# Differential attention's scores on two row halves of the array, memory heads' keys and values in two places

## The chip, the core and the metric

The kernel runs on one core of one Trainium2 chip. The metric is the device time of one execution in microseconds, median of the runs; the program is launched once and all its inputs lie in the chip's memory. Five engines work side by side: TensorE (PE in the profile, its weight loads PEld), VectorE (DVE), ScalarE (ACT), GpSimd (POOL) and SyncE (SP), which here issues most transfers. Each works through its own list of instructions in order and waits on semaphores for the others.

## What is computed

One step of a two-layer encoder with 1024 prompt frames and 32 sample frames, width 1024. Layer 0 mixes tokens by causal pooling, layer 1 by differential attention; each layer also attends, with four heads, to 256 memory tokens, and ends with a squared-ReLU feed-forward part of width 4096. The change is in layer 1. Its differential attention, four heads with two components of 64 dimensions each, in the reference:

```python
def diff_core(q, k, v, q_pos, k_pos, lam, slopes):
    s = jnp.einsum('bqhcd,bkhcd->cbhqk', q, k).astype(jnp.float32) * (DIFF_HEAD_DIM ** -0.5)
    dist = jnp.abs(q_pos[:, None] - k_pos[None, :]).astype(jnp.float32)
    bias = -slopes[:, None, None] * dist[None]
    vis = (k_pos[None, :] // CHUNK) <= (q_pos[:, None] // CHUNK)
    s = jnp.where(vis, s + bias, -jnp.inf)
    p = jax.nn.softmax(s, axis=-1)
    a = p[0] - lam * p[1]
    return jnp.einsum('bhqk,bkhe->bqhe', a.astype(v.dtype), v)
```

The memory attention is a plain softmax attention over 256 keys of 128 dimensions:

```python
def mem_attend(q, k, v):
    s = jnp.einsum('bthd,bmhd->bhtm', q, k).astype(jnp.float32) * (MEM_HEAD_DIM ** -0.5)
    p = jax.nn.softmax(s, axis=-1).astype(v.dtype)
    return jnp.einsum('bhtm,bmhd->bthd', p, v).reshape(B, T, MEM_WIDTH)
```

## The kernel before

Everything is held transposed: features on the 128 partitions, frames along the free dimension. The 1056 frames are three groups of 352 (`GW`). To keep accuracy, each operand of a matmul is split into a high part, rounded to the format F32R, and a low part, the rest (`split`, L56 and L57: a cast by ACT and a subtraction by DVE or POOL). A product is then three matmuls, high by high, low by high and high by low (`mm3`, L51 to L53).

Layer 1's attention is `mix1`. A main list of work (`diff_unit`, then `mem_unit`) is driven against a filler, `fill1`, which projects keys, values and queries of the coming heads; `drive` lets so much of the filler run after each step as the step's `yield` says, so that TensorE has dense matmuls while the softmax of a block is under way. The tile framework then sets the order on each engine.

Scores of differential attention (`diff_scores`): a head's 1024 queries come in 8 blocks of 128 (index `i`, two to a `pair`), against the first `Wi` keys, 256 to 1024. Before the change a component's 64 dimensions fill all 128 rows of the array: the tile KS holds, for component `c`, the high part of the keys on one half of the partitions and the low part on the other, and Q holds the queries' high part on both halves, and likewise the low part. Two matmuls of 128 rows (L799 and L800) so give all four products of the parts. The copies of Q on the other half are made by transfers issued by SP (L734), two for each 256 queries. Each component takes a score tile of its own (`sctile`, two banks of accumulator memory, two such tiles), one after the other, with a `yield` between. DVE adds the distance table and takes the minimum (L806), ACT takes the exponential (L808), ACT and DVE combine the two components (L779, L780); component 1 has a single buffer (`p1`).

`diff_values` transposes the combined probabilities in TensorE (L841), splits them (tiles aTh and aTl) and multiplies them with the split values V, three matmuls for each 128 keys in the order of `mm3`.

Memory heads (`mem_unit`): `mem_load_kv` loads a head's keys into `mkr`, splits them into `mk`, loads its values into the same `mkr` (named mvr), and splits them into `mv`. `mkr`, `mk` and `mv` have one place each. The matmuls on them are `sc<-mk,mq` and `mm<-aTh,mv` at L51 to L53.

The sample group has its own small attention (`diff_sample`): scores at L878 and L879 with 64 rows and 32 columns of the array, values at L902 (128 rows) and L903 (32 rows).

The functions that the change touches, with the profile's line numbers:

Of the kernel before, what the change touches and what calls it, by code (L numbers as in the profile page):

```python
# [9 lines left out]
F32 = mybir.dt.float32  # L10
F32R = mybir.dt.float32r
AF = mybir.ActivationFunctionType
ALU = mybir.AluOpType
# [3 lines left out]
SEQ = 1024  # L17
NS = 32
NT = SEQ + NS
GW = 352  # L20
# [7 lines left out]
SC_DIFF = 64.0 ** -0.5  # L28
# [7 lines left out]
KEYS_AT = 1  # L36
T2_AT, T_AT = 8, 20
# [5 lines left out]
class Kern:  # L43
# [211 lines left out]
    def setup_late(self, b):  # L255
        nc, t = self.nc, self.t
        self.dtab = b.tile([128, 1152], F32, name="dtab")
        self.dists = b.tile([128, 288], F32, name="dists")
        self.claim(b, (("os", 512, 2),))
        nc.sync.dma_start(self.dists, t["dists"])  # L260
# [75 lines left out]
    def mem_project(self, l, h, p, out, qs, gate=()):  # L336
        nc = self.nc
# [4 lines left out]
        for g in range(NG):  # L342
# [4 lines left out]
            for a, lo, hi in ((0, 0, 512), (1, 512, SEQ)):  # L347
                lo, hi = max(lo, g * GW), min(hi, (g + 1) * GW)
                if lo < hi:
                    s = slice(lo - 512 * a, hi - 512 * a)  # L350
                    self.split(q[a][:, 0, s], q[a][:, 1, s], qf[:, lo - g * GW:hi - g * GW], nc.gpsimd)
            if g == NG - 1:
                nc.gpsimd.tensor_copy(qs[:, h, :], qf[:, GW - NS:])
        out[h] = q

# [329 lines left out]
    def diff_project(self, h, p, out, smp):  # L685
        nc, t = self.nc, self.t
# [23 lines left out]
        Q = []  # L710
        for g in range(NG):
# [4 lines left out]
            lo, end = g * GW, min((g + 1) * GW, SEQ)  # L716
            if h:
                yield from self.until(("s", h - 1, (end - 1) // 256))
            while lo < end:
                n = lo // 256  # L720
                hi = min(end, 256 * (n + 1))
                s = slice(lo - 256 * n, hi - 256 * n)
                if len(Q) == n:
                    Q.append(self.qp.tile([128, 2, 2, 256], F32R, tag="q", name="Q", bufs=self.nq))
                q = Q[n]
# [13 lines left out]
    def diff_keys(self, h, smp):  # L739
# [6 lines left out]
        KSf = KS.bitcast(F32)  # L746
        for a in range(4):
            s = slice(256 * a, 256 * a + 256)
            nc.scalar.copy(KS[0:64, 0, s], kst[0:64, s])
            nc.scalar.copy(KS[64:128, 1, s], kst[64:128, s])  # L750
            nc.vector.tensor_tensor(KS[64:128, 0, s], kst[0:64, s], KSf[0:64, 0, s], ALU.subtract)
            nc.vector.tensor_tensor(KS[0:64, 1, s], kst[64:128, s], KSf[64:128, 1, s], ALU.subtract)
            yield 0.0
# [28 lines left out]
    def diff_scores(self, h, pair, p, d, A):  # L782
        nc = self.nc
        Wk = 256 * (pair + 1)
        q = d["Q"][pair]
        KS = self.KS[h]
        for i in (2 * pair, 2 * pair + 1):
            qc = slice((i % 2) * 128, (i % 2) * 128 + 128)
            Wi = max(256, 128 * (i + 1))
            st = self.pd.tile([128, 8], F32, tag="std", name="std", bufs=4)  # L790
            prs = []
            for c in range(2):
                tile = self.sctile()
                n = Wi if Wi <= 512 else Wi // 2
                off = 512 - n if Wi > 512 else 0
                sc = tile[:, off:off + Wi]
                for k in range(0, Wi, n):
                    o = sc[:, k:k + n]
                    nc.tensor.matmul(o, lhsT=q[:, c, 0, qc], rhs=KS[:, c, k:k + n], start=True, stop=False)  # L799
                    nc.tensor.matmul(o, lhsT=q[:, c, 1, qc], rhs=KS[:, c, k:k + n], start=False, stop=True)  # L800
# [10 lines left out]
                if c == 0:  # L811
                    yield 0.22 * (pair + 1)
# [868 lines left out]
```

## Time and profile before

| what | us |
|---|---|
| median of 3 runs | 2105.55 (2105.54 to 2108.3) |
| profiled execution, its own time | 2107.0 |
| span of its profile, first to last instruction | 2105.2 |
| TensorE busy in the span | 2081.7 (99%) |
| DVE, ACT, POOL busy | 1683.4, 1125.7, 568.0 |
| mean granted TensorE clock | 0.997 |
| layer 1's score matmuls, first start | 1015.6 |
| layer 1's score matmuls, last start | 1228.3 |
| memory heads' last value product of layer 1 | 1324.9 |

A row of the page's part on groups gives line, engine, operation, the tile written and those read, the form (rows x columns), the count, busy time and mean duration, and behind the last bar the idle time ahead of it with what ended it. The timeline gives start and duration of single instructions; in a matmul's row the form `64*32 64x256` reads: 64 rows and 32 columns of the array in use, 256 columns streamed. Matmul records overlap, so the pace is read from starts.

### The profile page before, as it was taken

To read this page: it belongs to the slowest core of one execution; us is meant where nothing else is said; L and a number is where in the kernel's file an instruction comes from. 1 tells how busy PE (TensorE), PEld (TensorE's weight loads), DVE (VectorE), ACT (ScalarE), POOL (GpSimd) and SP (SyncE) were. 2 spreads that over 40 slices of the span, in tenths; PEclk is the share of its full clock that TensorE was granted. 3 is DMA by queue.
4 is the path that set the end of the run, shared out by engine and by line. 5 is a ranking of instruction groups with operands and counts; after the bars stand their busy time and mean duration, and the time that the engine had idled before them with its cause. 6 is when DMAs were issued, how large, how long until landed. Compare 5 with 4: busy or idle time off the path is not lost. (4 is left out here: it accounts for less than half of the span.)

```text
span 2105.2 us, 35352 instructions
## 1 busy us (share of the span) xinstructions
PE 2081.7 (99%) x13068; PEld 2045.3 (97%) x13068; DVE 1683.4 (80%) x3164; ACT 1125.7 (53%) x2437; POOL 568.0 (27%) x577
## 2 busy tenths in 40 slices
PE   9999999999999999999999999999999999999998
PEld 8998999999999999999999998999999999999997
DVE  8856598888888888868778877589888888888865
ACT  7546365444444444456777766355544444444454
POOL 1021113333333333220111212104334333333323
PEclk9999999999999999999999999999999999999999
DMA  5634411111111111124222213411111111111112
GB/s 192 198 113 139 149 55 56 51 49 53 49 53 45 57 41 60 41 71 159 77 79 79 83 37 99 160 51 51 56 46 54 48 51 51 48 53 50 52 41 83
DMA packets 88269, 156.85 MB, mean 75 GB/s; under 512 B 12832, under 2 KB 30880, under 8 KB 87584
## 3 DMA queue, kind: packets, MB, share of 16 engines
q1 hardware_dynamic: 86224, 149.61, 22.3%
q10 hardware_dynamic: 1872, 4.98, 0.8%
q8 instruction: 102, 1.67, 0.3%
q14 instruction: 71, 0.58, 0.1%
HBM read 126.64 MB, written 23.72 MB: 71 GB/s over the span
## 5 line engine op out<-in xcount | busy, mean ns | idle before, releaser
L51 PE MATMUL dn<-xh,whi 128*128 128x352 f32 x1168 | 383.8, 329 | 2.9 <-ACT xh L229 1.1
L52 PE MATMUL dn<-xl,whi 128*128 128x352 f32 x1168 | 379.0, 324 | 0.4 <-DVE xl L230 0.4
L53 PE MATMUL dn<-xh,wlo 128*128 128x352 f32 x1168 | 378.9, 324 | 0.0
L109 DVE TENSOR_TENSOR wlo<-wraw,whi 128x512 fp32r<-128x512 f32 x344 | 280.1, 817 | 83.6 <-ACT whi L108 82.8
L1375 DVE TENSOR_TENSOR x<-x,mm 128x352 f32<-128x352 f32 x560 | 287.5, 513 | 62.7 <-PE mm L53 62.6
L108 ACT CAST whi<-wraw 128x512 fp32r<-128x512 f32 x344 | 212.4, 620 | 232.4 <-PE dn L52 117.5
L51 PE MATMUL mm<-h2h,whi 128*128 128x352 f32 x832 | 270.4, 325 | 0.0
L53 PE MATMUL mm<-h2h,wlo 128*128 128x352 f32 x832 | 268.0, 322 | 0.0
L52 PE MATMUL mm<-h2l,whi 128*128 128x352 f32 x832 | 266.4, 320 | 0.0
L108 ACT CAST whi<-ws 128x512 fp32r<-128x512 f32 x232 | 143.9, 620 | 220.3 <-PE dn L52 123.4
L1375 DVE TENSOR_TENSOR x<-x,xb 128x352 f32<-128x352 f32 x448 | 222.8, 511 | 26.1 <-PE xb L53 23.4
L51 PEld LDWEIGHTS dn<-xh,whi 128*128 128x128 f32 x1168 | 219.8, 188 | 8.4 <-issue 2.0
L52 PEld LDWEIGHTS dn<-xl,whi 128*128 128x128 f32 x1168 | 221.0, 189 | 3.1 <-DVE xl L230 1.3
L53 PEld LDWEIGHTS dn<-xh,wlo 128*128 128x128 f32 x1168 | 220.4, 189 | 0.4
L57 POOL TENSOR_TENSOR h2l<-t,h2h 128x352 fp32r<-128x352 f32 x112 | 137.0, 1224 | 170.8 <-ACT h2h L56 170.8
L109 DVE TENSOR_TENSOR wlo<-ws,whi 128x512 fp32r<-128x512 f32 x232 | 179.0, 772 | 3.5 <-ACT whi L108 3.5
L57 POOL TENSOR_TENSOR h2l<-b,h2h 128x352 fp32r<-128x352 f32 x92 | 116.2, 1275 | 228.7 <-PE mm L53 204.0
L1359 POOL TENSOR_TENSOR t<-b,b 128x352 f32<-128x352 f32 x56 | 64.7, 1155 | 366.3 <-ACT b L1278 366.3
L52 PEld LDWEIGHTS mm<-h2l,whi 128*128 128x128 f32 x832 | 156.3, 188 | 0.4
L51 PEld LDWEIGHTS mm<-h2h,whi 128*128 128x128 f32 x832 | 156.1, 188 | 0.4
L53 PEld LDWEIGHTS mm<-h2h,wlo 128*128 128x128 f32 x832 | 156.2, 188 | 0.0
L53 PE MATMUL dn<-T,wlo 128*128 128x352 f32 x480 | 155.7, 324 | 0.0
(312 smaller groups left out, 5326.9 us busy)
## 6 DMA issues: line engine op xcount, KB each, us to landing
wraw<-in_w_ff SPq DMA_DIRECT2D x256, 256.0 KB, 2.6
wraw<-in_w_out SPq DMA_DIRECT2D x44, 256.0 KB, 3.6
wraw<-in_w_mem SPq DMA_DIRECT2D x32, 256.0 KB, 3.1
wraw<-in_w_in SPq DMA_DIRECT2D x30, 256.0 KB, 3.1
o<-oscr SPq DMA_DIRECT2D x36, 176.0 KB, 3.0
xscr<-x SPq DMA_DIRECT2D x3, 1408.0 KB, 4.7
wraw<-in_w_kv SPq DMA_DIRECT2D x16, 256.0 KB, 2.6
Q<-Q SPq DMA_DIRECT2D x32, 128.0 KB, 2.2
```

Source lines behind the costliest of these rows:

```text
L51: mm(ps, lhsT=ah, rhs=bh, start=first, stop=False, skip_group_check=more)
L52: mm(ps, lhsT=ah, rhs=bl, start=False, stop=False, skip_group_check=more)
L53: self.last_mm = mm(ps, lhsT=al, rhs=bh, start=False, stop=last, skip_group_check=more)
L57: (lo_eng or self.nc.vector).tensor_tensor(lo, src, hi.bitcast(F32), ALU.subtract)
L108: self.nc.scalar.copy(hi, src)
L109: eng.tensor_tensor(lo, src, hi.bitcast(F32), ALU.subtract)
L1359: self.nc.gpsimd.tensor_tensor(h[out], h[a], h[c], ALU.subtract)
L1375: nc.vector.tensor_tensor(xj, xj, ps, ALU.add)
```

## The change

Each component's 64 dimensions now use one half of the array's rows: component 0 rows 0 to 63, component 1 rows 64 to 127. KS and Q hold high and low part as two planes of all 128 partitions, split like any other operand, by ACT and DVE in pieces of 512 columns for the keys, by ACT and POOL for the queries (`split_q`, which the memory queries use too). The copies of Q by SP are gone. A block has three matmuls of 64 rows a component (high by high, high by low, low by high), issued in turn for component 0 and 1, without a `yield` between. Up to 512 keys both components share a score tile, one bank each; above, both tiles are taken at once. A head's queries take two tiles of 512 and not four of 256, and the filler may be two heads ahead (`until` on head h - 2).

In `diff_values` the three products go by part: all that need the high part of the probabilities first. `mk` and `mv` have two places in layer 1 (`nmk`). The sample group's distance table is loaded where it is used and not ahead, and the weights of two `yield`s change (0.22 to 0.25).

```diff
+    def split_q(self, q, qf, g):
+        for a, lo, hi in ((0, 0, 512), (1, 512, SEQ)):
+            lo, hi = max(lo, g * GW), min(hi, (g + 1) * GW)
+            if lo < hi:
+                s = slice(lo - 512 * a, hi - 512 * a)
+                self.split(q[a][:, 0, s], q[a][:, 1, s], qf[:, lo - g * GW:hi - g * GW], self.nc.gpsimd)
...
     def diff_project(self, h, p, out, smp):
...
-        Q = []
+        if h > 1:
+            yield from self.until(("s", h - 2, 3))
+        Q = [self.qp.tile([128, 2, 512], F32R, tag="q", name="Q", bufs=self.nq) for a in range(2)]
...
-                for c in range(2):
-                    b = slice(64 * c, 64 * c + 64)
-                    self.split(q[b, c, 0, s], q[b, c, 1, s], qf[b, lo - g * GW:hi - g * GW], nc.gpsimd)
-                lo = hi
-                if hi == 256 * (n + 1):
-                    qd = q.bitcast(F32)
-                    for c in range(2):
-                        b, o = slice(64 * c, 64 * c + 64), slice(64 - 64 * c, 128 - 64 * c)
-                        nc.sync.dma_start(qd[o, c], qd[b, c])
+            self.split_q(Q, qf, g)
...
     def diff_keys(self, h, smp):
...
-        for a in range(4):
-            s = slice(256 * a, 256 * a + 256)
-            nc.scalar.copy(KS[0:64, 0, s], kst[0:64, s])
-            nc.scalar.copy(KS[64:128, 1, s], kst[64:128, s])
-            nc.vector.tensor_tensor(KS[64:128, 0, s], kst[0:64, s], KSf[0:64, 0, s], ALU.subtract)
-            nc.vector.tensor_tensor(KS[0:64, 1, s], kst[64:128, s], KSf[64:128, 1, s], ALU.subtract)
+        for a in range(0, SEQ, 512):
+            s = slice(a, a + 512)
+            self.split(KS[:, 0, s], KS[:, 1, s], kst[:, s])
...
     def diff_scores(self, h, pair, p, d, A):
...
+            n = Wi if Wi <= 512 else Wi // 2
+            if Wi > 512:
+                sc = [self.sctile()[:, 512 - n:512 - n + Wi] for c in range(2)]
+            else:
+                tile = self.sctile()
+                sc = [tile[:, 512 * c:512 * c + Wi] for c in range(2)]
+            for k in range(0, Wi, n):
+                for m, (u, v) in enumerate(((0, 0), (0, 1), (1, 0))):
+                    for c in range(2):
+                        b = slice(64 * c, 64 * c + 64)
+                        nc.tensor.matmul(sc[c][:, k:k + n], lhsT=q[b, u, qc], rhs=KS[b, v, k:k + n],
+                                         start=m == 0, stop=m == 2)
             prs = []
             for c in range(2):
-                tile = self.sctile()
...
-                for k in range(0, Wi, n):
-                    o = sc[:, k:k + n]
-                    nc.tensor.matmul(o, lhsT=q[:, c, 0, qc], rhs=KS[:, c, k:k + n], start=True, stop=False)
-                    nc.tensor.matmul(o, lhsT=q[:, c, 1, qc], rhs=KS[:, c, k:k + n], start=False, stop=True)
...
     def diff_values(self, h, pair, p, d, A):
...
-                for a in range(2):
-                    k = kk - 2 + a
-                    self.mm3(po, V[:, 0, k, :], V[:, 1, k, :], ah[:, 256 * a:256 * a + 256],
-                             al[:, 256 * a:256 * a + 256], k == 0, k == nk - 1)
+                for u, part in ((0, ah), (1, ah), (0, al)):
+                    for a in range(2):
+                        k = kk - 2 + a
+                        nc.tensor.matmul(po, lhsT=V[:, u, k, :], rhs=part[:, 256 * a:256 * a + 256],
+                                         start=kk == 2 and a == u == 0 and part is ah,
+                                         stop=kk == nk and part is al and a == 1)
...
     def mix1(self):
-        self.nq, self.nmk = 4, 1
+        self.nq, self.nmk = 4, 2
...
-        gates = [[("s", 3, 1)], [("s", 3, 3)], [("m", 1, 0, 1)], [("m", 1, 1, 1)]]
+        gates = [[("s", 2, 3)], [("s", 3, 3)], [("m", 1, 0, 1)], [("m", 1, 1, 1)]]
```

How the order moves, at three places. In the changed kernel the lines of `mm3` are L52 to L54, the score matmul is L784, the value products are L822. On PE, head 0's last block of queries (1024 keys, so two pieces of 512 for each component), before:

```order
L53 MATMUL dn<-xh_11248,wlo 128x352
L799 MATMUL sc<-KS,Q 128x512
L800 MATMUL sc<-KS,Q 128x512
L799 MATMUL sc<-KS,Q 128x512
L800 MATMUL sc<-KS,Q 128x512
L51 MATMUL dn<-xh_11248,whi 128x352
```

and in the changed kernel:

```order
L53 MATMUL dn<-xl_11249,whi 128x352
L54 MATMUL dn<-xh_11248,wlo 128x352
L784 MATMUL sc<-KS,Q 128x512 x12
L52 MATMUL dn<-xh_11248,whi 128x352
L53 MATMUL dn<-xl_11249,whi 128x352
```

The two groups of four, one for each component and twelve dense matmuls apart, have become one group of twelve, between dense matmuls of the next head's projection as before.

On PE, the third block of head 1 (384 keys) and what stands about it, in the changed kernel:

```order
L54 MATMUL dn<-xh_10905,wlo 128x352
L784 MATMUL sc<-KS,Q 128x384 x5
L822 MATMUL mm<-aTh,V 128x256 x4
L784 MATMUL sc<-KS,Q 128x384
L52 MATMUL dn<-xh_11086,whi 128x352
L822 MATMUL mm<-aTl,V 128x256 x2
```

A block's six matmuls can stand in two groups, here five and one, with value products between; the value products that need aTl stand behind all four that need aTh. In the whole order the score matmuls stand in 48 groups.

On SP, around the loads for memory head 3 (kscr_78 and vscr_86; kscr_77 and vscr_85 are head 2's, oscr_99 and oscr_100 the outputs of heads 0 and 1), before:

```order
L409 DMA oscr_99<-mo 128x512
L364 DMA mvr<-vscr_85 128x256
...
L409 DMA oscr_100<-mo 128x512
L1018 DMA o<-oscr_100 128x352
...
L409 DMA oscr_100<-mo 128x512
L359 DMA mkr<-kscr_78 128x256
```

and in the changed kernel:

```order
L367 DMA mvr<-vscr_85 128x256
...
L412 DMA oscr_99<-mo 128x512
L362 DMA mkr<-kscr_78 128x256
L1009 DMA o<-oscr_99 128x352
L412 DMA oscr_100<-mo 128x512
L367 DMA mvr<-vscr_86 128x256
```

Head 3's keys are asked for ahead of head 1's outputs and not behind them.

More of the change, by code (lines that the diff above doesn't have):

```diff
@@ L36 @@
 KEYS_AT = 1
+Y0, Y1 = 0.25, 0.25
 T2_AT, T_AT = 8, 20
@@ L346, in mem_project @@
             nc.vector.tensor_tensor(qf, ps, self.rs[g], ALU.mult)
[L347 to L351, printed above, removed]
+            self.split_q(q, qf, g)
             if g == NG - 1:
@@ L784, in diff_scores @@
         Wk = 256 * (pair + 1)
-        q = d["Q"][pair]
+        q = d["Q"][pair // 2]
         KS = self.KS[h]
         for i in (2 * pair, 2 * pair + 1):
-            qc = slice((i % 2) * 128, (i % 2) * 128 + 128)
+            qc = slice(128 * i - 512 * (pair // 2), 128 * i - 512 * (pair // 2) + 128)
             Wi = max(256, 128 * (i + 1))
             st = self.pd.tile([128, 8], F32, tag="std", name="std", bufs=4)
+            n = Wi if Wi <= 512 else Wi // 2
[10 more added lines that the diff above has]
+                                         start=m == 0, stop=m == 2)
             prs = []
             for c in range(2):
-                tile = self.sctile()
-                n = Wi if Wi <= 512 else Wi // 2
-                off = 512 - n if Wi > 512 else 0
-                sc = tile[:, off:off + Wi]
-                for k in range(0, Wi, n):
-                    o = sc[:, k:k + n]
-                    nc.tensor.matmul(o, lhsT=q[:, c, 0, qc], rhs=KS[:, c, k:k + n], start=True, stop=False)
-                    nc.tensor.matmul(o, lhsT=q[:, c, 1, qc], rhs=KS[:, c, k:k + n], start=False, stop=True)
                 if c:
@@ L805, in diff_scores @@
                 y = YOFF - 128 * i
-                nc.vector.tensor_tensor_reduce(out=pr[:, :Wi], in0=sc, in1=self.dtab[:, y:y + Wi], scale=-SC_DIFF,
+                nc.vector.tensor_tensor_reduce(out=pr[:, :Wi], in0=sc[c], in1=self.dtab[:, y:y + Wi], scale=-SC_DIFF,
                                                scalar=3e38, op0=ALU.add, op1=ALU.min, accum_out=st[:, c:c + 1])
@@ L811, in diff_scores @@
                 if c == 0:
-                    yield 0.22 * (pair + 1)
+                    yield Y0 * (pair + 1)
             nc.vector.reciprocal(st[:, 6:8], st[:, 4:6])
@@ L820, in diff_scores @@
                 self.done.add(("s", h, pair))
-            yield 0.22 * (pair + 1)
+            yield Y1 * (pair + 1)
     def diff_values(self, h, pair, p, d, A):
@@ L872, in diff_sample @@
         nc.scalar.dma_start(vc, t["cv"])
+        dists = p.tile([128, 288], F32, tag="os", name="dists", bufs=2)
+        nc.scalar.dma_start(dists, t["dists"])
         yield from self.wait(3)
@@ L944, in mix1 @@
             self.claim(self.pd, (("kst", NT, 1), ("vst", NT, 1), ("ks", 2 * SEQ, 2), ("v", 2 * SEQ, 1), ("pA2", 768, 2),
-                                 ("std", 8, 4), ("pad", 672, 1)))
+                                 ("std", 8, 4), ("pad", 224, 1)))
             self.claim(p, (("q", 1024, self.nq), ("qf", GW, 2), ("st", 16, 4), ("pA3", 1024, 2), ("aTh", 512, 2),
-                           ("aTl", 512, 2), ("mkr", 256, 1), ("mk", 512, 1), ("pad", 128, 1)))
+                           ("aTl", 512, 2), ("mkr", 256, 1), ("mk", 512, 2)))
             self.setup_late(p)
-            self.claim(p, (("mv", 512, 1), ("p1", 1024, 1), ("rs_y", 256, 1), ("rs_r", 256, 1), ("sq", 256, 1),
+            self.claim(p, (("mv", 512, 2), ("p1", 1024, 1), ("rs_y", 256, 1), ("rs_r", 256, 1), ("sq", 256, 1),
                            ("of", 256, 2)))
```

15 lines of the change are left out of this document (1 added, 14 removed).

## The prediction

> **What bounds the kernel now.** I read the page first, then stretches of the timeline, then the waits. The page says one engine fills the span:
>
> ```profile
> span 2105.2 us, 35352 instructions
> PE 2081.7 (99%) x13068; PEld 2045.3 (97%) x13068; DVE 1683.4 (80%) x3164; ACT 1125.7 (53%) x2437; POOL 568.0 (27%) x577
> ```
>
> A busy matmul need not stream at full pace, since the records overlap, so the timeline of layer 1's attention was read for the distance between starts. In each row stand the start in us, the duration, the engine, the line, the tiles and the form:
>
> ```profile
> 1047.60 0.32 PE L51 MATMUL dn<-xh,whi 128*128 128x352 f32 x1
> 1047.76 0.32 PE L52 MATMUL dn<-xl,whi 128*128 128x352 f32 x1
> ...
> 1048.07 0.40 PE L799 MATMUL sc<-KS,Q 128*128 128x512 f32 x1
> 1048.31 0.39 PE L800 MATMUL sc<-KS,Q 128*128 128x512 f32 x1
> 1048.54 0.39 PE L799 MATMUL sc<-KS,Q 128*128 128x512 f32 x1
> ```
>
> A product of 352 columns holds TensorE for 0.16 us, one of 512 for 0.23: 0.455 ns a column (0.16/352). Nothing lies between. What TensorE does wait for in all of this part is little (engine, line, releaser: total us, times, longest):
>
> ```profile
> PE sc L51 <- ACT mk L56: 1.7, 1, 1.7
> PE mm L52 <- DVE aTl L57: 0.7, 2, 0.4
> PE mm L772 <- DVE std L813: 0.6, 1, 0.6
> PE sc L51 <- ACT pr L551: 0.4, 1, 0.4
> PE sc L799 <- DVE std L806: 0.2, 1, 0.2
> PE sc L52 <- DVE mk L57: 0.2, 1, 0.2
> PE mm L51 <- ACT aTh L56: 0.2, 1, 0.2
> ```
>
> With a few below 0.2 that is some 4 us of 325 (1010 to 1335). So the change is worth what it does to TensorE's stream, plus at most 4 us.
>
> **Term 1: the score products, in columns.** Before:
>
> ```profile
> L799 PE MATMUL sc<-KS,Q x96: 278/346/527, 1015.8 to 1228.1; 128*128 128x384 f32 x24, 128*128 128x512 f32 x24, 128*128 128x256 f32 x16, 128*128 128x320 f32 x16
> ```
>
> The rest of the 96 (16) have 448 columns, and L800 repeats all. That is 2 x (24 x 384 + 24 x 512 + 16 x (256 + 320 + 448)) = 75,776 columns, 34.4 us. The change makes 3 products of 64 rows per component instead of 2 of 128: 288 instead of 192, 113,664 columns. Whether that is more or less hangs on whether the upper and lower half of the array stream at the same time. The old sample-group scores do this already: L878 uses rows 0 to 63 for component 0, rows 64 to 127 for component 1 (each such product is two records). In a window cut to their first two starts, and in a wider one:
>
> ```profile
> L878 PE MATMUL sc<-kvc,qsd x16: 376/388/400, 1236.3 to 1240.1; 64*32 64x256 f32 x16
> ...
> 1236.34 0.41 PE L878 MATMUL sc<-kvc,qsd 64*32 64x256 f32 x2
> ...
> 1236.34 0.63 PE L878 MATMUL sc<-kvc,qsd 64*32 64x256 f32 x4
> ```
>
> The first two, at most 0.400 long, lie within 0.41, and two more end 0.22 later: the halves run side by side. So the 113,664 columns take the time of 56,832, 25.8 us. The order leaves some halves alone: in heads 1 and 2 blocks are cut 5+1, 1+2+3 and 5+7, in head 3 3+3 and 4+1+1. Each cut leaves one half-product without partner: 2 x (384 + 512 + 320) x 0.455 ns = 1.1, and 0.3 for head 3. Sum 27.2: **-7.2 us**. Bounds: -8.6 (no loss at the cuts), and above it the case of no overlap, a rival below.
>
> **Term 2: going into 64 rows and out.** The same old products show what it costs when the form changes. In:
>
> ```profile
> 1239.42 0.28 PE L52 MATMUL sc<-mk,mq 128*128 128x256 f32 x1
> ...
> 1239.54 0.28 PE L53 MATMUL sc<-mk,mq 128*128 128x256 f32 x1
> 1239.75 0.17 PEld L878 LDWEIGHTS sc<-kvc,qsd 64*32 64x32 f32 x10
> ```
>
> and out:
>
> ```profile
> 1240.21 0.29 PE L879 MATMUL sc<-ksd,qsd 64*32 64x32 f32 x12
> ...
> 1240.42 0.19 PEld L53 LDWEIGHTS dn<-xh,wlo 128*128 128x128 f32 x1
> 1240.42 0.43 PE L53 MATMUL dn<-xh,wlo 128*128 128x352 f32 x1
> 1240.53 0.19 PEld L51 LDWEIGHTS dn<-xh,whi 128*128 128x128 f32 x1
> 1240.69 0.32 PE L51 MATMUL dn<-xh,whi 128*128 128x352 f32 x1
> 1240.85 0.32 PE L52 MATMUL dn<-xl,whi 128*128 128x352 f32 x1
> ```
>
> In a steady stream a weight load starts while the matmul before it streams, and costs nothing. Here the next load waits: 0.21 after the start of a matmul whose columns take 0.12, so TensorE drains for 0.09; then the load itself is bare. On the way out the first full-height load starts at 1240.42, the next at 1240.53, and the second matmul at 1240.69, 0.27 after 1240.42: 0.11 of load and 0.16 of columns. A switch thus costs 0.09 + 0.11 = 0.20 us.
>
> Is it the rows, or the 32 columns of these old products? L903 has 32 rows but all 128 columns:
>
> ```profile
> 1274.18 0.52 PEld L902 LDWEIGHTS mm<-dsT,kvc 128*128 128x128 f32 x4
> 1274.74 0.29 PEld L903 LDWEIGHTS mm<-dsT,vsd 32*128 32x128 f32 x2
> 1275.08 0.52 PEld L902 LDWEIGHTS mm<-dsT,kvc 128*128 128x128 f32 x4
> ```
>
> Six loads at 0.11 ((0.52 - 0.19)/3) would be 0.66 us; the round takes 0.90. Two switches cost 0.24, 0.12 each, in a chain whose loads are bare anyway. So height alone does it. Bounds per switch: 0.09 (the drain, next load hidden) and 0.12 + 0.11 = 0.23. I take 0.20, the dense case, nearest to what surrounds the scores. In the changed order of PE the score products stand in 48 separate stretches (32 blocks of a head's 128 queries, some cut), each between full-height products: 96 switches, **+19.2 us** (8.6 to 22.1). Before there were none here.
>
> The Trainium skill (TensorE: Matmul & The Clock Gate, section LDWEIGHTS) says a load's time goes by its columns and not its rows, 128/1.2 = 107 ns; the full-height 0.11 above agrees, and no run here shows a 64-row load of 128 columns. By it every load in a stretch still costs 0.11, under the 0.117 of the narrowest product, so the sum stays.
>
> **Term 3: waits that go.** The 1.7 us is memory head 3's keys:
>
> ```profile
> 1294.41 0.32 SPq L359 DMA_DIRECT2D mkr<-kscr  x1
> ...
> 1298.94 0.40 ACT L56 CAST mk<-mkr 128x256 fp32r<-128x256 f32 x1 [3.32 <-DMA mkr<-kscr]
> ```
>
> They land in the tile mkr, which head 2's values leave only when ACT and DVE have split them into the single mv, and that waits for head 1's last value product. With mk and mv in two places the split needn't wait; the new SP order has head 3's load ahead of both stores of head 1's outputs, and not behind them. -1.7. The value products now run all four with the high part first (0.47 us of stream) before the low part is needed, which covers both waits for aTl (0.4 at most): -0.7. The other waits keep their causes. **-2.4 us** (0 to -4).
>
> **Term 4: what lies beside TensorE.**
>
> ```profile
> L56 ACT CAST Q<-qf 64x256 fp32r<-64x256 f32 (+4 forms) x48 | 15.9, 332 | 11.3 <-DVE qf L715 10.4
> L749 ACT CAST KS<-kst 64x256 fp32r<-64x256 f32 x16 | 6.5, 403 | 8.2 <-DVE kst L694 8.1
> L751 DVE TENSOR_TENSOR KS<-kst,KS 64x256 fp32r<-64x256 f32 x16 | 6.7, 419 | 2.0 <-ACT KS L749 1.5
> ```
>
> ACT loses 32 key casts of 0.40 us (L750 is like L749) for 8 of 512 columns, and 48 query casts of 0.33 for 16; DVE loses 32 subtractions of 0.42 for 8; POOL works on whole tiles; 32 copies Q to Q leave SP's queue. None of these ended a listed wait of TensorE, whose stream covers them: 0. Were that cover gone, the 17 us or so that ACT saves (12.9 + 15.9 less 8 casts of 0.6 and 16 of 0.4) would count.
>
> One thing could be late next: above 512 keys a block takes both score tiles at once, so it waits for the previous block's second reduction (L806):
>
> ```profile
> L806 DVE CUSTOM_DVE_ANT_0 pr<-sc,dtab 128x768 f32<-128x768 f32 x8 | 7.6, 952 | 1.5 <-PE sc L800 1.5
> ```
>
> Two take 1.9 us, while the order puts 18 dense products, four transposes and one sum (2.9 + 0.4 + 0.3) between the blocks of 768 and 896 keys. 0; at worst 0.2 for each of 16 such blocks, 3 us. A stretch at half clock adds 1.5 us either way (clock 0.56 below); it may move or vanish:
>
> ```profile
> 1277.30:1281.10 3.80, 3.80 (x18) 3.72 (x17) 1.12 (x2) 2.25 (x5) 0.00 (x0) 0.56 0.28 104
> ```
>
> **Sum:** -7.2 + 19.2 - 2.4 = +9.6 us. On the profiled execution's span 2105.2 gives 2114.8 (its own time was 2107.0, 1.8 more); on the median of the runs, 2105.55, it gives **2115.1 us**. Its own range: 2108 (switch 0.15) to 2120 (switch 0.23, late reductions).
>
> **The rivals.**
> A. Row halves cost no switch: -7.2 - 2.4, 2096 us, faster. For it: inside L878's group nothing drains between the halves, 0.01 us apart by the durations above. Against it: the 0.21 and the 0.90 at each change of height. The point from which it decides: a switch below 9.6/96 = 0.10 us. The skill's page TensorE: Matmul & The Clock Gate (Part 3: Packing small matmuls) has packed products cost 4 ns each and nothing else, which is this rival; TensorEngine Tiling (Array Packing), section Key Properties, says a change of mode drains the engine. The rows side with the second.
> B. Only the drain is paid and the load is pulled ahead: 96 x 0.09 = 8.6, 8.6 - 9.6 = -1.0, 2104.5: no change. Against: both bare loads above.
> C. The two halves' loads go one after the other, 0.22 a pair. Then pairs below 480 columns go by loads: 0.10 more at 256, 0.07 at 320, 0.04 at 384, 0.01 at 448, and each stretch's second half starts 0.11 late. By the two gaps in a 6-stretch and five in a 12-stretch: 1.9 us a head, +7.5, 2122.5. For it: each load is 0.11 and a pair needs two. Against: the first four loads of L878 lie within 0.15 although one takes 0.10:
>
> ```profile
> L878 PEld LDWEIGHTS sc<-kvc,qsd x16: 102/104/106, 1236.3 to 1239.8; 64*32 64x32 f32 x16
> ...
> 1236.33 0.15 PEld L878 LDWEIGHTS sc<-kvc,qsd 64*32 64x32 f32 x4 [0.18 <-DVE rs_r L215]
> ```
>
> D. The halves don't overlap at all: 113,664 columns, 51.7 us, +17.3 + 19.2 - 2.4 = +34, 2139.6. Against: the 0.41 above.
>
> **How the numbers follow.** Forecast 0.62, A 0.14, B 0.11, C 0.10, D 0.03. A measurement here can tell 0.2%, 4.2 us, from no change. Faster is A with a corner of B, 0.15; the same is the rest of B and the forecast's lower corner (cheaper switches, all waits gone), 0.12; slower 0.73. The range 2103 to 2124 takes in B and C and leaves out A and D and some tail, 0.2.
>
> **What would show it.** Term 1: score products at 64*128, two starting within 0.02 us, the next pair 0.12 to 0.23 later; C if pairs of 256 are 0.22 apart. Term 2: ahead of each stretch a PEld row 0.09 after the columns end, and behind it a bare load; A and B if loads start while the last matmul streams. Term 3: no 1.7 us wait of sc on mk. Layer 0, the two feed-forward parts and the end should keep their lengths; if they don't, or if TensorE waits for L806's tiles, the argument is wrong.

## The result and the profile after

| kernel | median, us | ratio to the kernel before, 95% interval |
|---|---|---|
| before | 2105.86 (2105.54 to 2108.3, 4 runs) | |
| changed | 2120.41 (2118.45 to 2122.22, 4 runs) | 1.0066, 1.0049 to 1.0084 |

The change costs 14.5 us, where 9.6 were forecast. The profiled execution of the changed kernel took 2121.7 us. Its page begins:

```profile
span 2119.9 us, 35306 instructions
...
PE 2097.0 (99%) x13164; PEld 2044.4 (96%) x13164; DVE 1677.7 (79%) x3140; ACT 1108.3 (52%) x2381; POOL 551.5 (26%) x545
```

PE is as full as before, of a longer span, and all others are busy for less. The score products, in the view of the tile KS (count, shortest, median and longest duration in ns, first and last start):

```profile
L784 PE MATMUL sc<-KS,Q x288: 273/364/501, 1015.6 to 1243.8; 64*128 64x384 f32 x36, 64*128 64x512 f32 x36, 64*128 64x256 f32 x24, 64*128 64x320 f32 x24
```

One stretch of twelve products in the timeline, cut to its first two starts, then to four, then whole; the weight loads of the first cut stand below it:

```profile
1048.04 0.32 PE L54 MATMUL dn<-xh,wlo 128*128 128x352 f32 x1
1048.29 0.51 PE L784 MATMUL sc<-KS,Q 64*128 64x512 f32 x2
...
1048.29 0.18 PEld L784 LDWEIGHTS sc<-KS,Q 64*128 64x128 f32 x2 [0.22 <-issue]
...
1048.29 0.74 PE L784 MATMUL sc<-KS,Q 64*128 64x512 f32 x4
...
1048.29 1.67 PE L784 MATMUL sc<-KS,Q 64*128 64x512 f32 x12
1049.89 0.43 PE L52 MATMUL dn<-xh,whi 128*128 128x352 f32 x1
1050.16 0.32 PE L53 MATMUL dn<-xl,whi 128*128 128x352 f32 x1
```

Two products lie within 0.51 though one takes up to 0.50, and their two weight loads lie within the 0.18 of one: the halves run side by side and load side by side. The stretch begins 0.25 after the start of a matmul whose columns take 0.16: the drain of 0.09. Behind it the second dense product starts 0.27 after the first, 0.11 of bare load and 0.16 of columns. All of that was forecast. Not so this stretch in head 3, cut to one start, to two, and whole:

```profile
1232.30 0.32 PE L52 MATMUL dn<-xh,whi 128*128 128x352 f32 x1
1232.56 0.47 PE L784 MATMUL sc<-KS,Q 64*128 64x448 f32 x1
...
1232.56 0.67 PE L784 MATMUL sc<-KS,Q 64*128 64x448 f32 x2
...
1232.56 1.48 PE L784 MATMUL sc<-KS,Q 64*128 64x448 f32 x6
```

All six belong to one component: one half of the array streams, one product behind the other, and the other half stands empty. What TensorE waits for in the attention of layer 1 (engine, tile, line, releaser: total us, times, longest):

```profile
PE mm L822 <- DVE aTl L58: 3.4, 3, 1.2
PE mm L53 <- DVE aTl L58: 0.6, 1, 0.6
PE mm L210 <- ACT aTh L57: 0.3, 1, 0.3
```

The wait of 1.7 us on mk is gone, but those on aTl have grown from 0.7 to 4.0. One of the three long ones, in the timeline of DVE and PE:

```profile
1114.33 1.08 DVE L793 CUSTOM_DVE_ANT_0 pr<-sc,dtab 128x896 f32<-128x896 f32 x1
...
1115.02 0.64 PE L822 MATMUL mm<-aTh,V 128*128 128x256 f32 x4
...
1115.34 1.09 DVE L793 CUSTOM_DVE_ANT_0 pr<-sc,dtab 128x896 f32<-128x896 f32 x1
...
1116.35 0.69 DVE L58 TENSOR_TENSOR aTl<-mm,aTh 128x512 fp32r<-128x512 f32 x1
...
1117.09 0.50 PE L822 MATMUL mm<-aTl,V 128*128 128x256 f32 x2 [1.11 <-DVE aTl L58]
```

Both components of a block now end together, so their two reductions stand close behind each other on DVE: the second starts 0.36 us after the first ends (median of the 32 blocks), where it was 3.1 us in the kernel before. Here they take 2.0 us for 896 keys, and the subtraction that makes aTl stands behind them. The long wait in head 2 (1.14) looks the same; in head 0's (1.16) the subtraction stands behind a combination of probabilities (1.01) and one reduction (1.08).

**Where the 14.7 us of the two profiles lie.** From the starts of all matmuls I worked out three lengths for each kernel. The part is the time from the first score product to the 4200th matmul from the end, which lies in the feed-forward part. The windows are the sum over the stretches of score products, each from the end of the columns ahead of it to the beginning of the columns behind it. The rest is the part less the windows. The experiments' rows are put in here, to be looked up later. Each row is one profiled execution; the two of the changed kernel differ by 1.1 in the rest, so differences of that size say little.

| kernel | stretches | windows, us | rest, us | part, us |
|---|---|---|---|---|
| before | 69 (128 rows) | 38.2 | 361.2 | 399.5 |
| changed | 48 | 52.0 | 362.2 | 414.2 |
| changed, second time (e9) | 48 | 52.0 | 361.1 | 413.0 |
| e1, uncut and paired | 32 | 39.5 | 368.7 | 408.1 |
| e2, paired | 44 | 46.7 | 363.8 | 410.6 |
| e3, one component after the other | 32 | 46.6 | 364.0 | 410.5 |
| e7, as e1, split first | 32 | 41.3 | 365.0 | 406.3 |
| e8, as e7, two blocks together | 24 | 37.5 | 370.4 | 407.9 |
| e10, as e1, POOL combines | 32 | 41.2 | 382.2 | 423.4 |
| e4, the change without the scores | 66 (128 rows) | 38.8 | 359.9 | 398.7 |
| e11, e4 once more | 66 (128 rows) | 38.7 | 358.5 | 397.2 |
| e12, two places alone | 69 (128 rows) | 38.3 | 360.4 | 398.7 |

The part takes all of it. What comes behind (679.4 us) is the same in both, and what comes ahead differs by 0.2. The windows grew by 13.8 us: columns 34.4 to 25.8, -8.6; 48 stretches at 0.40, +19.2; halves without a partner and late first products, 52.0 - 25.8 - 19.2 = +7.0; and 3.8 us of waits and odd fractions in the windows of before are gone. Of the 7.0, 5.7 lie in 13 stretches that run longer than half their columns and 0.40: nine in head 3, the two of head 0's block of 640 keys, and one of 896 keys in each of heads 1 and 2. The other 1.3 are the cuts, which the forecast had at 1.4.

### The profile page after: what moved, and what is told of

Its sections match the earlier page's. It is cut to its first block, busy times and chain, and to the rows that moved or that the text cites. A ratio compares the mean times of both kernels' runs of the same rounds, so it can differ in the third digit from the quotient of the medians.

```text
span 2119.9 us, 35306 instructions
## 1 busy us (share of the span) xinstructions
PE 2097.0 (99%) x13164; PEld 2044.4 (96%) x13164; DVE 1677.7 (79%) x3140; ACT 1108.3 (52%) x2381; POOL 551.5 (26%) x545
## 3 DMA queue, kind: packets, MB, share of 16 engines
q8 instruction: 103, 1.69, 0.3%
## 4 chain that ended last, share of the span: by engine, by line
PE 89%; DVE 2%; ACT 2%; issue 1%; DMA 1%; POOL 0%; SPq 0%; DVEq 0%; ACTq 0%; POOLq 0%
PE dn L52 15%; PE dn L54 15%; PE dn L53 15%; PE mm L52 9%; PE mm L53 9%; PE mm L54 9%; PE xb L52 3%; PE xb L54 3%; PE xb L53 3%; PE sc L784 2%; PE mm L822 1%; PE sc L52 1%; PE sc L53 1%; PE sc L54 1%; PE mm L830 1%
## 5 line engine op out<-in xcount | busy, mean ns | idle before, releaser
L52 PE MATMUL dn<-xh,whi 128*128 128x352 f32 x1168 | 385.7, 330 | 2.8 <-DVE edge L603 1.0
L54 PE MATMUL dn<-xh,wlo 128*128 128x352 f32 x1168 | 379.1, 325 | 0.0
L52 PE MATMUL mm<-h2h,whi 128*128 128x352 f32 x832 | 270.3, 325 | 0.0
L54 PE MATMUL mm<-h2h,wlo 128*128 128x352 f32 x832 | 268.0, 322 | 0.0
L52 PEld LDWEIGHTS dn<-xh,whi 128*128 128x128 f32 x1168 | 219.5, 188 | 11.9 <-issue 6.0
L54 PEld LDWEIGHTS dn<-xh,wlo 128*128 128x128 f32 x1168 | 220.0, 188 | 0.5 <-issue 0.2
L52 PEld LDWEIGHTS mm<-h2h,whi 128*128 128x128 f32 x832 | 156.1, 188 | 0.4
L54 PEld LDWEIGHTS mm<-h2h,wlo 128*128 128x128 f32 x832 | 156.2, 188 | 0.0
L54 PE MATMUL dn<-T,wlo 128*128 128x352 f32 x480 | 155.7, 324 | 0.0
```

The lines of the kernel that those rows point to most:

```text
L52: mm(ps, lhsT=ah, rhs=bh, start=first, stop=False, skip_group_check=more)
L54: self.last_mm = mm(ps, lhsT=al, rhs=bh, start=False, stop=last, skip_group_check=more)
```

## The experiments

Theory S, with which I began: each stretch costs two switches, 0.40 us, the halves that stream alone cost 7.0 us, and both go straight to the end. Its first rival, W: the loss is in what is late elsewhere, and the order of the products is no cause.

**e1: each block in one uncut stretch, halves in turn.** Each product is queued behind the one before it, and all but the first move ahead in the order; the halves and the parts are taken in another order than in the changed kernel; the first of a block above 512 keys waits for the last reduction, so that both tiles are free.

```diff
-            for k in range(0, Wi, n):
-                for m, (u, v) in enumerate(((0, 0), (0, 1), (1, 0))):
-                    for c in range(2):
-                        b = slice(64 * c, 64 * c + 64)
-                        nc.tensor.matmul(sc[c][:, k:k + n], lhsT=q[b, u, qc], rhs=KS[b, v, k:k + n],
-                                         start=m == 0, stop=m == 2)
+            last = first = None
+            for k in range(0, Wi, n):
+                for m, (u, v) in enumerate(((1, 0), (0, 0), (0, 1))):
+                    for c in (1, 0):
+                        b = slice(64 * c, 64 * c + 64)
+                        with self.tc.issue_after(last.ins) if last else ExitStack(), \
+                                self.tc.high_priority(3000) if last else ExitStack():
+                            last = nc.tensor.matmul(sc[c][:, k:k + n], lhsT=q[b, u, qc], rhs=KS[b, v, k:k + n],
+                                                    start=m == 0, stop=m == 2)
+                        if first is None and Wi > 512 and self.last_red is not None:
+                            self.tc.add_manual_dep(last.ins, self.last_red.ins.name, mybir.DependencyInfo(
+                                mybir.DependencyClass.Sync, mybir.DependencyReason.DATA), reason="both tiles")
+                        first = first or last
...
```

> The changed kernel, with each block's 6 or 12 score products in one piece: they alternate between the two halves of the rows from the first to the last, nothing stands between them, and a block above 512 keys starts only when both its score tiles are free. 32 stretches instead of 48, no half alone. Theory S (the loss is 0.40 us of switches for each stretch, and 7.0 us of halves that stream without a partner): 7.0 + 16 x 0.40 = 13.4 us less than the changed kernel's 2120.4, so 2107.0. Rival W (the loss comes from the new form elsewhere: score tiles and probabilities that are late): the order of the products is no cause, 2120 or above, since waiting for both tiles can only hold TensorE up longer.

Measured: 2116.44 us, ratio 1.0042 (1.0029 to 1.0056) to a kernel before that here took 2107.04. The windows fell from 52.0 to 39.5, 12.5 of the 13.4 expected, so TensorE's side of theory S holds. But the part fell by 6.1 only: the rest grew by 6.5. The time lies between the two forecasts. The waits of e1:

```profile
PE mm L830 <- DVE aTl L58: 4.1, 6, 1.2
PE mm L398 <- DVE aTl L58: 1.3, 1, 1.3
PE sc L52 <- ACT mk L57: 0.6, 1, 0.6
PE mm L830 <- ACT aTh L57: 0.5, 1, 0.5
```

With four smaller ones they make 8.0 us, where the changed kernel has 4.3. Another 1.7 is a stretch at half clock, which by the records of the granted clock is 6.8 us long here and 3.4 there. That is 5.4 of the 6.5; what the other 1.1 is stays open. So "straight to the end" is wrong: half of what TensorE's score windows save is lost again in the rest, most of that in waits and at half clock.

**e2: in pairs, but cuts allowed.** As e1 without the line with `high_priority`.

> As e1, the halves alternate and a block above 512 keys waits for both tiles, but other products may stand between a block's products, as in the changed kernel: 44 stretches. Theory S: of the 7.0 us of halves alone 1.3 stay (where a cut falls inside a pair), and 4 stretches fewer save 1.6: 7.3 us under the changed kernel, 2113.1. If only the number of switches counts and lone halves cost nothing: 2118.8. If lone halves are the whole loss: the same as e1.

Measured: 2119.40 us, 1.0060 (1.0046 to 1.0074). The windows fell by 5.3 (7.3 expected; two of its stretches hold a wait of some 0.7), the part by 3.6, and the time by an amount that the intervals can't tell from nothing. The time is near 2118.8, the forecast in which lone halves cost nothing, but not for that reason: the windows did fall. By itself, pairing the halves brings little of what the windows promise.

**e3: one component after the other.** As e1, with the loops in another order:

```diff
-            for k in range(0, Wi, n):
-                for m, (u, v) in enumerate(((1, 0), (0, 0), (0, 1))):
-                    for c in (1, 0):
+            for c in (1, 0):
+                for k in range(0, Wi, n):
+                    for m, (u, v) in enumerate(((1, 0), (0, 0), (0, 1))):
```

> As e1, 32 stretches in one piece, but all products of component 1 first and then all of component 0, so that no two halves stand side by side. Theory S: every product streams alone, 25.8 us more than e1, 2132.8. If the halves share the time no better when they alternate: the same as e1.

Measured: 2117.01 us, 1.0046 (1.0030 to 1.0061), as e1 and not 2132.8. The main reason is in the timeline, six products of 256 columns issued three for component 1 and then three for component 0, cut to the first 0.17 us and then whole:

```profile
1080.13 0.39 PE L788 MATMUL sc<-KS,Q 64*128 64x256 f32 x2
...
1080.13 0.63 PE L788 MATMUL sc<-KS,Q 64*128 64x256 f32 x6
```

Two have started within 0.17 us, and six are done in 0.63, where one after the other they would take 0.70 of columns alone: by the order of the program, TensorE takes the fourth product, for the free half, past the second and third. The starts bear it out: in e1, where the halves alternate, the two of a pair start 3 to 4 ns apart, here the first two start 10 ns apart. In stretches of 12, six and six, the first product of the second half starts, by the starts of the twelve, together with the third, 0.40 after the first for pieces of 320 columns and 0.57 for 512: it passes three products and not six. The windows are 46.6 and not the 64.5 that lone halves would take. In the changed kernel there is nothing to pass: the six products of the other component stand behind dense ones or value products, of full height.

The windows are still 7.1 us longer than e1's, and the time is not, for in the profiles the rest is 4.7 shorter. The waits on aTl in the differential heads, 4.1 us in e1, are less here:

```profile
PE mm L830 <- DVE aTl L58: 0.8, 3, 0.4
```

The two kernels differ only in the order within a stretch. So these waits hang on when a block's components end, as theory Q below says.

**e5 and e6: the price of a switch by itself.** The kernel before, with 84 products of a tile of zeros in the dense projections, in e5 over 64 rows, in e6 over 128.

```diff
-            yield from self.g_dense(ps, W, g)
+            for c, _ in enumerate(self.g_dense(ps, W, g)):
+                if c < C - 1:
+                    nc.tensor.matmul(ps[:, :256], lhsT=self.zero[:ROWS, :], rhs=self.xh[g][:ROWS, c, :256],
+                                     start=False, stop=False)
+                yield 0.45
...
```

> The kernel before, with 84 extra products in the dense projections of layer 1's keys (7 in each of 4 heads x 3 groups), each behind a full-height low-part product: rows 0 to 63 of a tile of zeros by 256 columns, added to the running sum. Each is a stretch of 64 rows between full-height products. Theory S: 0.116 us of columns and two switches at 0.20 each, 0.516 x 84 = 43.3 us more than before. Rival A (height alone costs nothing): 9.8 us more. Rival B (only the drain, 0.09 each): 24.9 us more.

> As e5, the same 84 products in the same places, but over all 128 rows of the zeros. All theories: 84 x 0.116 = 9.8 us more than before. The difference to e5 is 168 switches and nothing else: 33.6 us by theory S.

Measured: 2169.24 us, ratio 1.0289 (1.0267 to 1.0311), and 2124.20, 1.0076 (1.0055 to 1.0096), over 2107.10. In the timeline of e5, and then of e6, one round of three dense products and one of zeros:

```profile
1108.72 0.38 PE L696 MATMUL dn<-xh,zero 64*128 64x256 f32 x1
1109.03 0.43 PE L52 MATMUL dn<-xh,whi 128*128 128x352 f32 x1
1109.30 0.32 PE L53 MATMUL dn<-xl,whi 128*128 128x352 f32 x1
1109.46 0.32 PE L54 MATMUL dn<-xh,wlo 128*128 128x352 f32 x1
1109.71 0.38 PE L696 MATMUL dn<-xh,zero 64*128 64x256 f32 x1
```

```profile
1079.52 0.28 PE L696 MATMUL dn<-xh,zero 128*128 128x256 f32 x1
1079.63 0.33 PE L52 MATMUL dn<-xh,whi 128*128 128x352 f32 x1
1079.80 0.32 PE L53 MATMUL dn<-xl,whi 128*128 128x352 f32 x1
1079.96 0.32 PE L54 MATMUL dn<-xh,wlo 128*128 128x352 f32 x1
1080.12 0.28 PE L696 MATMUL dn<-xh,zero 128*128 128x256 f32 x1
```

A round takes 0.99 us with the low product and 0.60 with the full one: 0.39 for two switches, 0.195 each, where the forecast had 0.20. From the dense product ahead of the zeros to the second one behind them, the medians over the 84 are 0.832 and 0.439, 0.393 apart. Rivals A and B of the prediction are refuted. In the times both runs carry more than their dose: 62.1 and 17.1 us over before, where 43.3 and 9.8 were forecast. Each waits some 5 us for the tile of zeros, and a stretch at half clock follows, 6.8 us in e6 and 41 us in e5, where a round takes 1.69 us. Of the 45.0 us between their times, 84 x 0.393 = 33.0 are switches; the other 12.0 lie within what 34 us more at half clock can cost, 17.

**e7: the split ahead of the reductions.** By then e1 and the timeline of the changed kernel spoke for theory Q: what the scores save on TensorE is lost to waits on DVE. The test was e1 with the transposes and the split of the probabilities moved ahead in the order:

```diff
+PRI = 400
...
-                for a in range(2):
+                with self.tc.high_priority(PRI):
+                    for a in range(2):
...
-                self.split(ah, al, pt)
+                    self.split(ah, al, pt)
```

> As e1 (32 uncut, paired stretches), and the transposes of the probabilities and the split into aTh and aTl stand earlier in the order, so that on DVE the subtraction for aTl mostly goes ahead of, or between, a block's two reductions of scores. Theory Q (what e1 saved on TensorE's scores it lost to waits on DVE, whose two reductions of a block now come right behind each other and hold up the split): the waits on aTl in the differential heads, 4.1 us in e1, go: about 4 us under e1, 2112.4 where before is 2107.0. Rival (the waits move to the reductions, and so to the score tiles): as e1, 2116.

Measured: 2114.74 us, 1.0035 (1.0024 to 1.0046), 1.7 under e1, with intervals that overlap, and between its two forecasts. The row that should have gone is there:

```profile
PE mm L840 <- DVE aTl L59: 4.1, 6, 0.8
```

All listed waits make 6.0 us, where e1 has 8.0. The stretch at half clock is 3.4 us here and 6.8 in e1, which by itself is worth the 1.7. So moving the split ahead did not take the waits away, only made the longest shorter (0.8, from 1.2).

**e8: two blocks in one stretch up to 512 keys.** As e7, with the products of both blocks of the first two pairs ahead of their softmax, 24 stretches. One thing more changes: the first product of a stretch waits for the last reduction at any number of keys, and not only above 512.

```diff
+            if i not in scs:
+                last = first = None
+                for e in (2 * pair, 2 * pair + 1) if pair < 2 else (i,):
...
+                                if first is None and self.last_red is not None:
```

> As e7, and up to 512 keys both blocks of a pair go in one stretch, each in one of the two score tiles: 24 stretches. Theory S: 8 stretches fewer, 8 x 0.40 = 3.2 us under e7. Rival Q2 (four reductions that become ready together hold up the splits, as the two did in e1): not under e7, and more waits on aTh or aTl in the rows of TensorE's waits.

Measured: 2117.03 us, 1.0043 (1.0026 to 1.0060). The windows fell by 3.8, and the rest grew by 5.4:

```profile
PE mm L847 <- DVE aTl L59: 4.8, 7, 1.1
```

Both signs of rival Q2 came: the time is not under e7's, and there is more waiting on aTl. But that row grew by 0.7 only, all listed waits by 2.7 (6.0 to 8.7), and the other 2.7 of the rest stay open; how much the added wait for the last reduction does isn't separated. Fewer switches alone don't pay here.

**e10: POOL combines the probabilities.** As e1, to take 16 instructions of some 1.1 us off DVE:

```diff
-        nc.vector.scalar_tensor_tensor(p0[:P, :W], p0[:P, :W], r0, p1[:P, :W], ALU.mult, ALU.subtract)
+        if W > 512:
+            nc.gpsimd.tensor_scalar(p0[:P, :W], p0[:P, :W], r0, 1.0, ALU.mult, ALU.mult)
+            nc.gpsimd.tensor_tensor(p0[:P, :W], p0[:P, :W], p1[:P, :W], ALU.subtract)
+        else:
+            nc.vector.scalar_tensor_tensor(p0[:P, :W], p0[:P, :W], r0, p1[:P, :W], ALU.mult, ALU.subtract)
```

> As e1 (32 uncut, paired stretches), and above 512 keys POOL and not DVE combines the two components' probabilities (a scaling and a subtraction in place of one instruction; 16 blocks, about 1.1 us each off DVE). Theory Q (e1's gain went to DVE, whose two reductions of a block run right behind each other and hold up the split for aTl): the waits on aTl, 4.1 us in e1, fall to 1.5 or less, and the time to about 2.5 us under e1's, a ratio to before of 1.003. Rival (POOL's longer way makes the probabilities late instead): waits of the transposes on the probabilities, and no gain.

Measured: 2130.36 us, 1.0107 (1.0093 to 1.0120), 14 us over e1. From its waits, its groups on POOL, and its timeline (the second row is the fourth of five weight splits, shown alone):

```profile
PE mm L834 <- DVE aTl L58: 9.2, 5, 3.5
```

```profile
L766 POOL TENSOR_TENSOR pr<-pr 128x640 f32<-128x640 f32 (+3 forms) x15 | 29.5, 1968 | 6.8 <-ACT pr L763 6.8
```

```profile
1040.52 0.86 DVE L115 SCALAR_TENSOR_TENSOR wlo<-wraw,gains,whi 128x128 fp32r<-128x128 f32 x3
...
1041.30 1.93 DVE L115 SCALAR_TENSOR_TENSOR wlo<-wraw,gains,whi 128x128 fp32r<-128x128 f32 x1
...
1041.17 1.90 POOL L766 TENSOR_TENSOR pr<-pr 128x768 f32<-128x768 f32 x1 [1.58 <-ACT pr L763]
...
1043.42 1.08 DVE L805 CUSTOM_DVE_ANT_0 pr<-sc,dtab 128x896 f32<-128x896 f32 x1
1044.42 1.08 DVE L805 CUSTOM_DVE_ANT_0 pr<-sc,dtab 128x896 f32<-128x896 f32 x1
1045.43 0.68 DVE L58 TENSOR_TENSOR aTl<-mm,aTh 128x512 fp32r<-128x512 f32 x1
1046.17 0.63 PE L834 MATMUL mm<-aTl,V 128*128 128x256 f32 x2 [3.52 <-DVE aTl L58]
```

The remedy failed: the waits on aTl went from 4.1 to 9.2. The timeline shows why TensorE stands for 3.5 us. Of five weight splits on DVE four take 0.34 each, but the fourth, which starts 0.13 after a subtraction on POOL, takes 1.93 and ends 0.15 after it; then come a fifth split and two reductions, and only then the subtraction for aTl. Six weight splits of this run, this one among them, take 1.8 to 2.0 us, and each ends 0.15 after such a subtraction. So the edit brought a delay of its own to DVE, one that neither rival had, and e10 does not test theory Q alone: the queue that Q names is there, but behind a held split.

Nor are the waits all of it. The stretches at half clock make 20.5 us in e10 and 6.8 in e1, worth 6.8 us; all listed waits make 14.1 us against 8.0. That is 12.9 of the 13.5 by which the rest grew.

**e9: the changed kernel once more**, beside e10.

> The changed kernel once more, beside the kernel before and e10 on the same chip, so that e1 (ratio 1.0042 to the kernel before) and it are read on one footing. Theory S and Q: a ratio of 1.0066 as at first, about 14 us over before; were it 1.0042, uncutting and pairing would have brought nothing.

Measured: 2120.82 us, 1.0063 (1.0049 to 1.0077). It repeats the first result. The interval of e1 (up to 1.0056) overlaps this one (from 1.0049), and that of e7 lies below it (up to 1.0046): the two remedies of e7 together do make the change cheaper, by about 6 us, and it stays slower than before.

**e4, e11 and e12: the change without the scores.** In e4 the kernel before takes over the two places, the order of the value products and the late distances, and keeps its scores, KS and Q, and also the old weights of the `yield`s and the old look-ahead of the filler; e11 is the same again; in e12 the value products keep their old order too.

```diff
-        self.nq, self.nmk = 4, 1
+        self.nq, self.nmk = 4, 2
...
-                           ("aTl", 512, 2), ("mkr", 256, 1), ("mk", 512, 1), ("pad", 128, 1)))
+                           ("aTl", 512, 2), ("mkr", 256, 1), ("mk", 512, 2)))
...
-            self.claim(p, (("mv", 512, 1), ("p1", 1024, 1), ("rs_y", 256, 1), ("rs_r", 256, 1), ("sq", 256, 1),
+            self.claim(p, (("mv", 512, 2), ("p1", 1024, 1), ("rs_y", 256, 1), ("rs_r", 256, 1), ("sq", 256, 1),
...
```

> The kernel before with all of the change but the scores: two places for the memory heads' keys and values, the value products with the high part first, the sample group's distances loaded late. Scores, KS and Q as before. Theory S: the waits on mk (1.7 us and 0.2) and on aTl (0.7) go, nothing is switched: 2.4 us under the kernel before, 2103.5. Rival V (the changed kernel's new waits on aTl, 3.4 us, come from the new order of the value products): the gain of 1.9 is eaten, 2105.9 - 1.9 + 3.4 - 0.7 = 2106.7.

> e4 once more (the kernel before with all of the change but the scores), since its ratio of 0.9993, 0.9985 to 1.0002, leaves open whether it gains. By the trace of e4, where neither a wait on mk nor one over 0.3 us on aTl is left: 2 us under before, ratio 0.999. Rival: 1.000.

> The kernel before with the two places for the memory heads' keys and values and the late distances alone; the value products in their old order. By the waits of before: the 1.7 and 0.2 us on mk go, the 0.7 on aTl stay: 1.9 us under before, and 0.7 over e11. Rival: the same as e11, since the new order's gain is covered elsewhere.

Measured: e4 0.9993 (0.9985 to 1.0002), e11 2104.52 us, 0.9986 (0.9977 to 0.9995), e12 2106.37 us, 0.9992 (0.9983 to 1.0001). The three longest waits of e11:

```profile
PE mm L770 <- DVE std L811: 0.6, 1, 0.6
PE sc L797 <- DVE std L804: 0.4, 1, 0.4
PE mm L52 <- DVE aTl L57: 0.3, 1, 0.3
```

Nothing on mk is left, and with the new order of the value products no value product of the differential heads (L833) waits for aTl; the 0.3 is in the memory heads. So the new order is not what made the changed kernel wait for aTl, and rival V falls. e4 and e11 are one kernel, the fastest here: 1.4 us under before, which is not clear of none, and then 2.6 (1.1 to 4.8). Whether the new order brings any of it can't be told: e4, e11 and e12 have intervals that overlap. In e12 a wait of 0.2 on mk is left, which the forecast had gone. No run separates the new `yield` weights and the look-ahead from the new scores.

## Why the prediction was right, and where it was off

**Direction and mechanism** were right: 96 switches cost more than the halves side by side and the waits give back, 14.5 us against 9.6 forecast, inside the range of 2103 to 2124.

**Term 1, the score columns (-7.2), is the step that failed.** Its overlap is there: 25.8 us is what the columns take where both halves stream, and the pairs start 3 to 4 ns apart. Rival D is refuted, and C too: the second and third pair of 256 start 0.12 apart, not 0.22 (only from a stretch's first pair to its second is it 0.22, where the bare load of the switch lies). The mistake is in the sentence that the order leaves some halves alone, with its list of cuts. The cuts cost what it says, about 1.3. But the list lacks the 13 stretches in which the order puts all products of one component together, or lets the halves run half a product apart. The order showed them, for instance in head 0, where the names are two score tiles:

```
L784 MATMUL sc_11962<-KS_11814,Q_11699 128x320 (six times)
L822 MATMUL mm_11979<-aTh_11948,V_11832 128x256 (four times)
L822 MATMUL mm_11979<-aTl_11949,V_11832 128x256 (two times)
L52 MATMUL dn_11932<-xh1_11248,whi_11688 128x352
L784 MATMUL sc_11963<-KS_11814,Q_11699 128x320 (six times)
```

I counted lengths of stretches there and not whose tile each product writes. The trace has these products in this order, the score products one after the other from 1026.17 and from 1028.43 us on. With them the term is -8.6 + 7.0 = -1.6, 5.6 us off.

**Term 2, the switches (+19.2), was right**: 48 stretches with 0.39 to 0.41 each where they are paired, and 0.195 for one switch in e5 against e6.

**Term 3, the waits that go (-2.4).** As a part of its own it was right: e4 and e11 are 1.4 and 2.6 us under before, and in the changed kernel the wait on mk is gone. The waits on aTl went the other way, 0.7 to 4.0, and not by the order of the value products (e4, e11). What made up for it are waits and odd fractions inside the windows of before, 3.8 us, among them the 0.6 on std, which I had left to "the other waits keep their causes".

**Term 4 (0)** named the right danger and the wrong victim. It priced both tiles taken at once by TensorE's wait for the second reduction, 3 us at worst. That wait hardly came; in the view of KS, among what its matmuls waited for (total us, times):

```profile
  DVE std L793: 0.6, 3
```

What waits is the split for aTl, three times 1.1 to 1.2 us, twice behind both reductions and once behind a combination and one reduction. A stretch at half clock, which the term had at 1.5 us, costs 1.7, half of its 3.4; it neither moved out of the part nor vanished.

The size of the miss, 4.9 us, is thus accounted for by the trace: -1.6 in Term 1, +19.2 as forecast, and -2.8 of waits (-3.8 in the windows, +1.0 in the rest) make 14.8, where the two profiles lie 14.7 apart. That the waits came so near to the -2.4 of the forecast is luck: two things that it didn't have, the new waits on aTl and the waits in the windows of before, nearly cancel. But e1, e2 and e8 show that such a sum doesn't run backwards: 12.5 us taken out of the score windows gave 6.1 in the part, and 14.5 gave 6.3. The missing half is shown to lie in the rest; that DVE's queue is its cause is shown for the waits on aTl, in the timelines and by e3, and argued beyond them, since the two remedies (e7, e10) did not take them away.

The other signs came out as stated: the parts ahead and behind keep their lengths, and there is no 1.7 us wait on mk.

## What to carry to other kernels

Price a half-height form by the number of stretches between full-height products, two switches each, before its columns, and read from the order of the program whose half each product uses, not just how many stand together. Work that one engine saves by doing two things at once arrives at the next engine at once too: look at what stands in that queue behind the pair. Where a change has an independent part that only takes a wait away, measure that part alone; here it was the only one that brought a gain, of 1.4 to 2.6 us.

## What the runs showed of the hardware that I had not expected

**Products of one half pass products of the other.** In e3 the fourth product in the program's order starts 10 ns after the first. The Trainium skill (TensorE: Matmul & The Clock Gate, section Step-by-step: what each phase is for) says that only weight loads are pulled ahead and matmuls stay in program order. The trace of e3 disagrees for two halves of the rows: 0.63 us for six products of 256 columns issued three and three.

**A switch** costs 0.195 us here, of which 0.09 is the drain by the starts shown above. The Trainium skill (TensorEngine Tiling (Array Packing), section Key Properties) says that changing the tiling mode drains the engine. The runs agree, and add a bare weight load each time.

**The clock.** Every profile has a stretch at half clock in the memory heads' part, 3.4 us or twice that, by the records of the granted clock. Here are the two windows around it in the kernel before, and those in e10 around the wait shown above (columns: window, its length, busy time and number of instructions of PE, PEld, DVE, ACT and POOL, granted clock, DMA share, GB/s):

```profile
1274.30:1277.70 3.40, 3.40 (x23) 3.02 (x24) 1.21 (x3) 0.63 (x3) 0.84 (x2) 1.00 0.00 0
1277.80:1281.20 3.40, 3.40 (x16) 3.33 (x15) 1.12 (x2) 1.81 (x4) 0.00 (x0) 0.50 0.31 116
```

```profile
1043.00:1046.40 3.40, 0.23 (x2) 0.23 (x3) 3.11 (x7) 1.87 (x3) 0.22 (x2) 1.00 0.23 77
1046.40:1049.80 3.40, 3.40 (x13) 3.40 (x13) 0.91 (x3) 2.02 (x5) 2.07 (x2) 0.50 0.00 0
```

In e10 the wait of 3.5 us is followed by 3.4 us at half clock, so it costs half as much again. From the starts, at 0.455 ns a column, I worked out for all fourteen profiles how much of each such window's time the columns fill, leaving out the first 12 us and the last 30. A window at full clock ahead of a drop has 0.03 (e10, above) to 0.36; the kernel before, whose products there have few columns, has 0.26. Windows at full clock with 0.45 and more were followed by none. So here products of few columns count as a rest, though PE is listed as busy for all of the 3.40. In e5, where each fourth product is of half height, a drop that lasts 6.8 us in e6 lasted 41 us. The Trainium skill (TensorE: Matmul & The Clock Gate, section What's actually happening) has a free-running window of 3413 ns and half rate after an idle one. The lengths agree; the kernel before shows that the window need not be idle.
